# Row softmax on one core: one 192 KB array, loads of 3, 5, 8 and then 16 rows, stores of mostly 8 and at the end 16 rows, and the first two loads at the program's head on two queues

## The chip, the cores and the metric

One NeuronCore of a Trainium2 chip runs the kernel. DVE (VectorE) and ACT (ScalarE) compute. SP (SyncE) and ACT issue transfers, each on a queue of its own, and the core's 16 DMA engines carry them out. The metric is the device time of one execution in microseconds (us). All runs quoted are marked fast in the record, with the clock at 1.0. The kernel before took 162.68 us (median of 3 runs, 162.29 to 162.74).

## The reference

A softmax over the last dimension of an array of 16 x 1024 rows of 512 float32 values, 33.55 MB in and as much out:

```python
def reference(x: np.ndarray) -> np.ndarray:
    x_max = np.max(x, axis=-1, keepdims=True)
    exp_x = np.exp(x - x_max)
    return (exp_x / np.sum(exp_x, axis=-1, keepdims=True)).astype(np.float32)
```

Laid over 128 partitions, each partition has 128 rows of 2 KB. "Rows" below means rows per partition: a chunk of 8 rows is 128 x 8 x 2 KB = 2 MB.

## The kernel before

Sixteen chunks of 8 rows, twelve tiles. Each chunk goes through DVE (negated row maximum), ACT (exponential with that bias, and the row sum), DVE (reciprocal, then one scaling per row), and is stored. SP's queue issues the loads, ACT's queue the stores. The first load stands at the program's head, ahead of the start barrier.

```python
CHUNKS = [8] * 16
SLOTS = {8: 12}
# ... (first_load_at_the_head moves the first load before the barrier)
    def load(k):
        R = CHUNKS[k]
        tiles[k] = data.tile([P, R, d], F32, name=f"x{R}", tag=f"x{R}", bufs=SLOTS[R])
        nc.sync.dma_start(out=tiles[k], in_=src[k])
# ... rowmax(k): one reduce_max over the chunk;  exps(k): one activation per row
    def scale(k):
        R = CHUNKS[k]
        recip = stats.tile([P, R], F32, name=f"recip{R}", tag=f"recip{R}")
        nc.vector.reciprocal(out=recip, in_=sums[k])
        for r in range(R):
            nc.vector.tensor_scalar_mul(
                out=tiles[k][:, r, :], in0=tiles[k][:, r, :], scalar1=recip[:, r : r + 1])

    def store(k):
        nc.scalar.dma_start(out=dst[k], in_=tiles[k])

    with tc.manual_schedule():
        for k in range(K):
            load(k)
            rowmax(k)
            exps(k)
            if k >= 1:
                scale(k - 1)
                store(k - 1)
        scale(K - 1)
        store(K - 1)
```

## Time and profile before

| kernel before | value |
|---|---|
| time, median | 162.68 us |
| span of the profiled run | 160.6 us |
| DVE / ACT busy | 77% / 58% of the span |
| DMA engines busy (two queues) | 49.7% + 48.8% = 98.5% of 16 engines' span |
| bytes moved | 67.1 MB, 418 GB/s over the span |

From the page of the kernel before: the span; the busy time of the engines; the busy tenths of DVE and of the DMA engines in 40 slices of 4 us; the GB/s of each slice; the two queues (packets, MB, share of 16 engines' span; q1 is SP's queue, q10 is ACT's); and the chain that ended last, by engine.

```profile
span 160.6 us, 527 instructions
...
DVE 123.8 (77%) x160; ACT 93.2 (58%) x257; POOL 0.2 (0%) x4
...
DVE  0098799999999999885960089999999999967000
...
DMA  7999999999999999999999999999999999999993
GB/s 233 441 424 428 441 420 371 437 430 428 428 433 433 430 424 437 437 420 437 424 437 441 420 432 428 433 439 420 428 433 432 441 428 424 433 433 437 424 433 167
...
q1 hardware_dynamic: 2304, 33.56, 49.7%
q10 hardware_dynamic: 2304, 33.56, 48.8%
...
DMA 52%; DVE 31%; ACT 7%; SPq 1%; issue 1%; ACTq 0%; DVEq 0%
...
```

Read the DMA row first. It is 9 (90% or more) from the second slice to the last but one: the DMA engines are hardly ever without work. That is a bound, whatever the chain of waits says. DVE has 31% of the chain, but its row shows it idle in the middle of the program (the digits 8859600) while DMA stayed at 9.

The trace's packet records say how the engines spend this time. A packet is one contiguous run of one partition, here 16 KB, and 2048 packets per queue take 611 ns each (median). 16 engines x 16384 B / 611 ns is 429 GB/s, and 256 packets per engine are 156.4 us of the span of 160.6.

The two ends of the program, before. From the timeline, the first work on DVE (start, duration, engine, line, operation, operands, and in brackets the idle time before it and what ended it):

```profile
...
7.72 4.42 DVE L73 TENSOR_REDUCE shift<-x 128x8 f32<-128x4096 f32 x1 [7.72 <-DMA x<-in_x_dram]
```

From the DMA view of the stretch after 148 us, the last store (KB, us from issue to landing). It was issued at 149.0:

```profile
...
out_dram<-x ACTq DMA_DIRECT2D x1, 2048.0 KB, 10.8
```

Its 2 MB are 8 packets per engine, 4.9 us, yet it took 10.8 us. The rest is mostly older stores in line before it.

### The profile page before, as it was taken

The numbers are of one execution on the slowest core, as the hardware profiler recorded it, in microseconds if no ns is written. First come the engines' busy times: TensorE is split into PE (matmuls) and PEld (weight loads), VectorE is DVE, ScalarE is ACT, GpSimd is POOL, SyncE is SP. The second block draws the span as 40 slices with busy tenths as digits, with TensorE's granted clock in tenths as the row PEclk, the third lists the DMA queues.
The fourth block names the chain that finished last, engine by engine and source line by source line (L and its number), as shares of the span: only waits on it lengthen the run. The fifth ranks groups of instructions, "written<-read, shape, count | busy, mean of one in ns | idle before, by whom it ended". The sixth has DMA issues, their size and how long they took to land.

```text
span 160.6 us, 527 instructions
## 1 busy us (share of the span) xinstructions
DVE 123.8 (77%) x160; ACT 93.2 (58%) x257; POOL 0.2 (0%) x4
## 2 busy tenths in 40 slices
DVE  0098799999999999885960089999999999967000
ACT  0029985867777685076002987859595959592000
POOL 0000000000000000000000000000000000000000
DMA  7999999999999999999999999999999999999993
GB/s 233 441 424 428 441 420 371 437 430 428 428 433 433 430 424 437 437 420 437 424 437 441 420 432 428 433 439 420 428 433 432 441 428 424 433 433 437 424 433 167
DMA packets 4611, 67.14 MB, mean 418 GB/s; under 512 B 512, under 2 KB 512, under 8 KB 512
## 3 DMA queue, kind: packets, MB, share of 16 engines
q1 hardware_dynamic: 2304, 33.56, 49.7%
q10 hardware_dynamic: 2304, 33.56, 48.8%
q14 instruction: 3, 0.02, 0.0%
HBM read 33.55 MB, written 33.55 MB: 418 GB/s over the span
## 4 chain that ended last, share of the span: by engine, by line
DMA 52%; DVE 31%; ACT 7%; SPq 1%; issue 1%; ACTq 0%; DVEq 0%
DMA x<-in_x_dram 52%; DVE shift L73 16%; DVE x L93 14%; ACT x L79 7%; SPq L68 1%; DVE recip L91 1%; ACTq L100 0%; DVEq L137 0%; ACTq L79 0%
## 5 line engine op out<-in xcount | busy, mean ns | idle before, releaser
L79 ACT ACTIVATE x<-x,shift 128x512 f32<-128x512 f32 x128 | 90.5, 708 | 44.5 <-DVE shift L73 21.0
L73 DVE TENSOR_REDUCE shift<-x 128x8 f32<-128x4096 f32 x16 | 70.6, 4414 | 9.1 <-DMA x<-in_x_dram 9.1
L93 DVE TENSOR_SCALAR x<-x,recip 128x512 f32<-128x512 f32 x128 | 52.1, 481 | 0.6
L79 ACT ACTIVATION_READ_ACCUMULATOR x<-x,shift 128x1 f32 x128 | 23.9, 187 | 0.0
L91 DVE RECIPROCAL recip<-sums 128x8 f32<-128x8 f32 x16 | 3.1, 195 | 15.5 <-ACT x L79 15.5
L79 ACT ACT_TABLE_LOAD x1 | 1.3, 1283 | 7.8 <-DMA x<-in_x_dram 7.8
L126 POOL MEMSET const-bfloat16-1.0<- 128x1 bf16 x1 | 0.1, 101 | 0.0
L126 POOL MEMSET const-uint8-127<- 128x1 uint8 x1 | 0.1, 101 | 0.0
L126 POOL MEMSET const-float32-0.0<- 128x1 f32 x1 | 0.1, 98 | 0.2 <-issue 0.2
L126 POOL MEMSET const-float32-1.0<- 128x1 f32 x1 | 0.1, 98 | 0.0
## 6 DMA issues: line engine op xcount, KB each, us to landing
x<-in_x_dram SPq DMA_DIRECT2D x16, 2048.0 KB, 42.9
out_dram<-x ACTq DMA_DIRECT2D x16, 2048.0 KB, 17.7
```

The costliest lines, as they stand in the source:

```text
L68: nc.sync.dma_start(out=tiles[k], in_=src[k])
L73: nc.vector.reduce_max(out=shift[k], in_=tiles[k], axis=AX, negate=True)
L79: nc.scalar.activation(out=tiles[k][:, r, :], in_=tiles[k][:, r, :], func=EXP, bias=shift[k][:, r : r + 1], scale=1.0, accum_out=sums[k][: ...
L91: nc.vector.reciprocal(out=recip, in_=sums[k])
L93: nc.vector.tensor_scalar_mul(out=tiles[k][:, r, :], in0=tiles[k][:, r, :], scalar1=recip[:, r : r + 1],)
L126: nc = _bacc.Bacc("TRN2", target_bir_lowering=False, num_devices=1)
```

## The change

The intent: let compute begin sooner on a small first load, move more bytes per transfer and per packet once it runs, and start both queues at the program's head. All data lie in one array of 96 rows (192 KB per partition). Eight loads are issued at once (3, 5, 8, then five of 16 rows), and the last two 16-row loads reuse rows after the stores of earlier chunks. Compute still goes by groups of up to 8 rows. Three of the 16-row chunks are stored in halves; the last four are stored whole. The first three chunks are finished one after the other.

```diff
-CHUNKS = [8] * 16
-SLOTS = {8: 12}
+CHUNKS = [
+    (3, 0), (5, 3), (8, 8), (16, 16), (16, 32), (16, 48), (16, 64), (16, 80), (16, 0), (16, 16),
+]
+SBUF_ROWS = 96
+EARLY = 8
+AFTER_STORE = {2: [8], 3: [9]}
+GROUP = 8
+FINISH_BEFORE = (1, 2, 3)
+STORE_ROWS = {3: 8, 4: 8, 5: 8}
+ON_ACT = (0,)
+AT_HEAD = {mybir.EngineType.Activation: 1, mybir.EngineType.SP: 1}
...
     def load(k):
-        R = CHUNKS[k]
-        tiles[k] = data.tile([P, R, d], F32, name=f"x{R}", tag=f"x{R}", bufs=SLOTS[R])
-        nc.sync.dma_start(out=tiles[k], in_=src[k])
+        queue = nc.scalar if k in ON_ACT else nc.sync
+        queue.dma_start(out=place[k], in_=src[k])
...  (rowmax, exps and scale work on a group (k, a, b) of rows of place[k] in the same way)
+        if since is not None:
+            nc.scalar.dma_start(
+                out=dst[k][:, since:b, :], in_=place[k][:, since:b, :]
+            )
+        if b == CHUNKS[k][0]:
+            for later in AFTER_STORE.get(k, ()):
+                load(later)
...
+        for k in range(EARLY):
             load(k)
-            rowmax(k)
-            exps(k)
-            if k >= 1:
-                scale(k - 1)
-                store(k - 1)
-        scale(K - 1)
-        store(K - 1)
+        waiting = None
+        for g, (k, a, _, _) in enumerate(groups):
+            if waiting is not None and a == 0 and k in FINISH_BEFORE:
+                scale(waiting)
+                waiting = None
+            rowmax(g)
+            exps(g)
+            if waiting is not None:
+                scale(waiting)
+            waiting = g
+        scale(waiting)
```

More of the change, by code (lines that the diff above doesn't have):

```diff
@@ L10, with loads_at_the_head @@
 AX = mybir.AxisListType.X
-CHUNKS = [8] * 16
-SLOTS = {8: 12}
-def first_load_at_the_head(nc):
-    main, body = nc.main_func.blocks[0], nc.main_func.blocks[1]
-    dmas = [i for i in body.instructions if type(i).__name__ == "InstDMACopy"]
-    load = dmas[0]
-    assert load.engine == mybir.EngineType.SP
-    body.instructions.remove(load)
-    barrier = next(
-        n
-        for n, i in enumerate(main.instructions)
-        if i.engine == mybir.EngineType.SP and type(i).__name__ == "InstDrain"
-    )
-    main.instructions.insert(barrier, load)
+CHUNKS = [
[9 more added lines that the diff above has]
+AT_HEAD = {mybir.EngineType.Activation: 1, mybir.EngineType.SP: 1}
+def loads_at_the_head(nc):
+    main, body = nc.main_func.blocks[0], nc.main_func.blocks[1]
+    for engine, count in AT_HEAD.items():
+        loads = [
+            i
+            for i in body.instructions
+            if i.engine == engine and type(i).__name__ == "InstDMACopy"
+        ][:count]
+        barrier = next(
+            n
+            for n, i in enumerate(main.instructions)
+            if i.engine == engine and type(i).__name__ == "InstDrain"
+        )
+        for load in loads:
+            body.instructions.remove(load)
+        main.instructions[barrier:barrier] = loads
 @with_exitstack
@@ L40 @@
     nc = tc.nc
-    nc.at_finalize(first_load_at_the_head)
+    nc.at_finalize(loads_at_the_head)
     P = nc.NUM_PARTITIONS
@@ L46 @@
     n, d = x_flat.shape
-    assert n == P * sum(CHUNKS)
+    assert n == P * sum(R for R, _ in CHUNKS)
     src, dst, at = [], [], 0
-    for R in CHUNKS:
+    for R, _ in CHUNKS:
         for flat, views in ((x_flat, src), (out_flat, dst)):
@@ L58 @@
     stats = ctx.enter_context(tc.tile_pool(name="stats", bufs=4))
-    K = len(CHUNKS)
-    tiles = [None] * K
-    shift = [None] * K
-    sums = [None] * K
-    def load(k):
-        R = CHUNKS[k]
-        tiles[k] = data.tile([P, R, d], F32, name=f"x{R}", tag=f"x{R}", bufs=SLOTS[R])
-        nc.sync.dma_start(out=tiles[k], in_=src[k])
-    def rowmax(k):
-        R = CHUNKS[k]
-        shift[k] = stats.tile([P, R], F32, name=f"shift{R}", tag=f"shift{R}")
-        nc.vector.reduce_max(out=shift[k], in_=tiles[k], axis=AX, negate=True)
@@ L75, in exps @@
-    def exps(k):
-        R = CHUNKS[k]
-        sums[k] = stats.tile([P, R], F32, name=f"sums{R}", tag=f"sums{R}")
-        for r in range(R):
+    held = data.tile([P, SBUF_ROWS, d], F32, name="held")
+    place = [held[:, s : s + R, :] for R, s in CHUNKS]
+    groups = []
+    for k, (R, _) in enumerate(CHUNKS):
+        m = max(1, round(R / GROUP))
+        cuts = [R * i // m for i in range(m + 1)]
+        since = 0
+        for a, b in zip(cuts, cuts[1:]):
+            ends = b == R or b - since >= STORE_ROWS.get(k, R)
+            groups.append((k, a, b, since if ends else None))
+            since = b if ends else since
@@ new lines, with rowmax, exps @@
+    shift = [None] * len(groups)
+    sums = [None] * len(groups)
+    def load(k):
+        queue = nc.scalar if k in ON_ACT else nc.sync
+        queue.dma_start(out=place[k], in_=src[k])
+    def rowmax(g):
+        k, a, b, _ = groups[g]
+        shift[g] = stats.tile([P, b - a], F32, name="shift", tag="shift")
+        nc.vector.reduce_max(
+            out=shift[g], in_=place[k][:, a:b, :], axis=AX, negate=True
+        )
+    def exps(g):
+        k, a, b, _ = groups[g]
+        sums[g] = stats.tile([P, b - a], F32, name="sums", tag="sums")
+        for r in range(a, b):
@@ L79, in exps, with scale @@
             nc.scalar.activation(
-                out=tiles[k][:, r, :],
-                in_=tiles[k][:, r, :],
+                out=place[k][:, r, :],
+                in_=place[k][:, r, :],
                 func=EXP,
-                bias=shift[k][:, r : r + 1],
+                bias=shift[g][:, r - a : r - a + 1],
                 scale=1.0,
-                accum_out=sums[k][:, r : r + 1],
+                accum_out=sums[g][:, r - a : r - a + 1],
             )
-    def scale(k):
-        R = CHUNKS[k]
-        recip = stats.tile([P, R], F32, name=f"recip{R}", tag=f"recip{R}")
-        nc.vector.reciprocal(out=recip, in_=sums[k])
-        for r in range(R):
+    def scale(g):
+        k, a, b, since = groups[g]
+        recip = stats.tile([P, b - a], F32, name="recip", tag="recip")
+        nc.vector.reciprocal(out=recip, in_=sums[g])
+        for r in range(a, b):
@@ L93, in scale @@
             nc.vector.tensor_scalar_mul(
-                out=tiles[k][:, r, :],
-                in0=tiles[k][:, r, :],
-                scalar1=recip[:, r : r + 1],
-            )
-    def store(k):
-        nc.scalar.dma_start(out=dst[k], in_=tiles[k])
+                out=place[k][:, r, :],
+                in0=place[k][:, r, :],
+                scalar1=recip[:, r - a : r - a + 1],
+            )
+        if since is not None:
+            nc.scalar.dma_start(
+                out=dst[k][:, since:b, :], in_=place[k][:, since:b, :]
+            )
@@ L102 @@
+        if b == CHUNKS[k][0]:
+            for later in AFTER_STORE.get(k, ()):
+                load(later)
     with tc.manual_schedule():
-        for k in range(K):
+        for k in range(EARLY):
             load(k)
-            rowmax(k)
-            exps(k)
-            if k >= 1:
-                scale(k - 1)
-                store(k - 1)
-        scale(K - 1)
-        store(K - 1)
+        waiting = None
[8 more added lines that the diff above has]
+            waiting = g
```

## The prediction

> **What bounds it now.** The DMA engines, from start to end. Each works off one packet after another; a 16 KB packet takes 611 ns in the trace's packet records (16 x 16384 B / 611 ns = 429 GB/s). The 67.1 MB are 256 such packets per engine: 156.6 us of a span of 160.6. The page's slices agree: DMA busy 9 in all but the first and last, 420 to 440 GB/s except in slice 1 (233), 7 (371) and 40 (167). The Trainium skill ("DMA: Bandwidth & Descriptors", section "Where 436 GB/s comes from") gives 435 GB/s as the ports' ceiling; the trace has 98% of it. DVE (123.8 us busy, 77%) and ACT (58%) have slack. DVE is on the chain of waits (31%) only because the last stores queue: the last is issued at 149.0 and lands after 10.8 us, 4.9 of them its own transfer, so about 6 us of older stores lay before it.
>
> What is left to win is 160.6 - 156.6 = 4.0 us: about 1.0 before the first packet, 0.8 lost by slow first packets (0.9 to 1.9 us each), 0.5 at 22 to 26 us where the first store starts, 0.2 of instruction fetches, 0.3 of 512 semaphore packets, 1.1 after the last data.
>
> **What the change does.**
> - It moves the same bytes. 16-row loads have 32 KB runs per partition. An 8 KB packet takes 307 ns, a 16 KB one 611: a fixed cost of about 3 ns. 88 packets fewer per engine save 0.3 us at most; 9 semaphore packets fewer, at 9 ns, 0.1 us.
> - The 3-row load: first reduce at 4 to 5 us instead of 7.7. That helps DVE, which is not the bound.
> - Two queues at the head: the second load was issued at about 1 us, long before the first (4.9 us of transfer) was through. Nothing waited for it. The skill's section "Issuing engines are not separate DMA queues" says both queues run on the same 16 engines; the trace agrees (alternating packets, sum 429 GB/s). To be won is part of the 0.5 us that ACT's queue cost at its first use, if it was the queue and not the writing: I count 0.2.
> - 16-row stores at the end: the last needs 9.8 us, so it must be issued by about 149 or the DMA engines run dry. Working through the new order with measured durations (reduce 4.35 us and scales 3.4 per 8 rows, ACT 0.70 per row, the queues' packets in turn) I get loads done at about 111 us, DVE done at 145, the last store issued there and landing after some 14 us. No gap in DMA, 4 us of margin.
> - Waits for reused semaphores: one store of the sixth chunk waits for a load that DVE needs then anyway.
>
> **On the critical path:** 0.3 + 0.1 + 0.2 us, so about 162.2 us, range 161.2 to 163.4. Faster by over 2% would need under 159.4: less than the 156.6 us of packets plus 1.0, 1.1 and the 2 us between span and time. Faster 2%, same 95%, slower 3%.
>
> **What would show it.** DMA at 9 in all middle slices, 425 to 440 GB/s; first reduce at 4 to 5 us; DVE still 124 us busy but done by 142 to 148; 32 KB packets of about 1220 ns; the last store issued about 145 and landing after 13 to 15 us.
>
> **What would make it wrong.** A hole in DMA: at the end, if DVE falls 4 us behind (loads coming later because stores take a larger share), or while loads 9 and 10 wait for stores of the first four chunks. Larger packets that run below 429 GB/s. A start that costs more with small packets of 6 and 10 KB on two queues.

## The result

| | before | after |
|---|---|---|
| time, median of 4 runs | 162.55 us | 162.76 us |
| lowest to highest | 162.29 to 162.74 | 162.70 to 162.78 |
| span of the profiled run | 160.6 us | 161.0 us |

The ratio is 1.0013, with a 95% interval of 0.9996 to 1.0031: the same. A ratio here is the mean time of one kernel's fast runs over the mean of the other's fast runs of the same rounds, so it is not quite the ratio of the medians quoted.

The same lines of the page, of the changed kernel:

```profile
span 161.0 us, 516 instructions
...
DVE 123.9 (77%) x162; ACT 93.3 (58%) x257; POOL 0.2 (0%) x4
...
DVE  0048287079969999999999999999999999958000
...
DMA  7999999999999999999999999999999999996996
GB/s 254 430 489 391 421 417 391 449 398 481 409 411 458 456 391 436 409 476 415 440 415 464 432 423 419 456 389 423 444 468 399 464 440 399 456 448 277 391 391 261
...
q10 hardware_dynamic: 2016, 34.34, 49.8%
q1 hardware_dynamic: 1296, 32.77, 48.1%
...
DVE 71%; ACT 14%; DMA 5%; issue 2%; DVEq 0%; ACTq 0%
...
```

Two things differ. The chain is now 71% DVE. And the DMA row, which had no gap before, has two 6s near its end, with 277 GB/s in the slice of 144 to 148 us. The engines ran dry there. The table of stretches shows it more sharply. Its columns are the stretch, its length, the busy us of DVE, ACT and POOL with their instruction counts, the clock, the DMA share and GB/s (a packet is counted where it starts). First before, then after:

```profile
...
10.00:146.00 136.00, 118.53 (x153) 91.89 (x256) 0.00 (x0) 1.00 1.01 429
146.00:150.00 4.00, 2.96 (x8) 0.00 (x0) 0.00 (x0) 1.00 1.00 426
...
```

```profile
...
10.00:146.00 136.00, 119.64 (x155) 92.04 (x257) 0.00 (x0) 1.00 1.01 432
146.00:150.00 4.00, 2.97 (x8) 0.00 (x0) 0.00 (x0) 1.00 0.67 287
...
```

Up to 146 us the changed kernel is a little ahead. Counting each packet by the part of it that lies before a given time, the records have 61.73 MB moved by 146 us before and 61.96 MB after. Between 146 and 150 us it loses this and more: by 150 us it is 63.46 MB against 62.96. In the records the engines run out of packets one after the other between 148.0 and 149.0, and start again between 149.8 and 150.0 us.

The last store of the changed kernel, also issued at 149.0:

```profile
...
out_dram<-held ACTq DMA_DIRECT2D x1, 4096.0 KB, 11.1
```

This one line points to the hole. Twice the bytes need 8 x 1213 ns (the median of a 32 KB packet) = 9.7 us, and it took 11.1, of which 0.85 passed between the issue and its first packet. Nothing lay before it. In the kernel before, a store half as large took as long because it stood in line.

DVE therefore finished too late for a store of that size, though it is no later than before (both issue the last store at 149.0). The prediction had it finish at 145. The start shows why it did not. Timeline of the changed kernel, all engines (ACTq is the issue of a transfer on ACT's queue):

```profile
...
0.12 0.38 ACTq L96 DMA_DIRECT2D held<-in_x_dram  x1
...
8.72 1.75 DVE L101 TENSOR_REDUCE shift<-held 128x3 f32<-128x1536 f32 x1 [8.72 <-DMA held<-in_x_dram]
...
```

The first load has 3 rows instead of 8, and yet DVE starts at 8.72 us, later than the 7.72 of before. The DMA view of the first 9 us shows what became of it (queues: packets, MB, share; then issues: KB, us from issue to landing):

```profile
...
q1 hardware_dynamic: 209, 2.38, 70.2%
q10 hardware_dynamic: 144, 0.79, 21.0%
...
held<-in_x_dram SPq DMA_DIRECT2D x1, 1280.0 KB, 7.0
held<-in_x_dram ACTq DMA_DIRECT2D x1, 768.0 KB, 8.6
```

The first load's 0.79 MB on ACT's queue took 8.6 us. The packet records show two parts of this. It was issued at 0.12 us, but its first packet moved only at 2.68, while SP's queue began at 1.00 and had the engines alone until then (the DMA view from 0 to 2.6 us lists no packet of q10):

```profile
...
q1 hardware_dynamic: 40, 0.41, 64.5%
```

From then on the queues took turns, and its packets needed 5.0 us. SP's queue moved 2.38 MB in the first 9 us: the 5-row load and half of the 8-row load. The 5-row load landed first.

### The profile page after: what moved, and what is told of

Read it like the earlier page. It is cut to its first block, busy times and chain, and to the rows that moved or that the text cites. A ratio compares the mean times of both kernels' runs of the same rounds, so it can differ in the third digit from the quotient of the medians.

```text
span 161.0 us, 516 instructions
## 1 busy us (share of the span) xinstructions
DVE 123.9 (77%) x162; ACT 93.3 (58%) x257; POOL 0.2 (0%) x4
## 4 chain that ended last, share of the span: by engine, by line
DVE 71%; ACT 14%; DMA 5%; issue 2%; DVEq 0%; ACTq 0%
DVE shift L101 39%; DVE held L123 30%; ACT held L109 14%; DMA held<-in_x_dram 5%; DVE recip L121 2%; DVEq L175 0%; ACTq L109 0%
## 5 line engine op out<-in xcount | busy, mean ns | idle before, releaser
L109 ACT ACTIVATE held<-held,shift 128x512 f32<-128x512 f32 x128 | 90.5, 708 | 43.4 <-DVE shift L101 31.2
L101 DVE TENSOR_REDUCE shift<-held 128x8 f32<-128x4096 f32 (+2 forms) x17 | 70.6, 4160 | 8.7 <-DMA held<-in_x_dram 8.7
L123 DVE TENSOR_SCALAR held<-held,recip 128x512 f32<-128x512 f32 x128 | 52.2, 480 | 0.6
L109 ACT ACTIVATION_READ_ACCUMULATOR held<-held,shift 128x1 f32 x128 | 23.9, 187 | 0.0
L121 DVE RECIPROCAL recip<-sums 128x8 f32<-128x8 f32 (+2 forms) x17 | 3.3, 193 | 15.8 <-ACT held L109 15.8
## 6 DMA issues: line engine op xcount, KB each, us to landing
held<-in_x_dram SPq DMA_DIRECT2D x1, 2048.0 KB, 11.5
```

The lines of the kernel that those rows point to most:

```text
L101: nc.vector.reduce_max(out=shift[g], in_=place[k][:, a:b, :], axis=AX, negate=True)
L109: nc.scalar.activation(out=place[k][:, r, :], in_=place[k][:, r, :], func=EXP, bias=shift[g][:, r - a : r - a + 1], scale=1.0, accum_out=s ...
L121: nc.vector.reciprocal(out=recip, in_=sums[g])
L123: nc.vector.tensor_scalar_mul(out=place[k][:, r, :], in0=place[k][:, r, :], scalar1=recip[:, r - a : r - a + 1],)
```

## The experiments

All ran with five rounds beside the kernel before on the same chip, except the seventh (three); e5 left four times. e1 to e4 shared one chip, e5 to e8 a second, e9 and e10 a third, and the changed kernel was measured earlier, in rounds of its own with the kernel before. The kernel before had medians of 162.52, 162.50 and 162.29 us there, so across these groups compare the ratios. "e1" is called the repaired kernel below. The theory after the traces was this. The DMA engines bound both kernels. The changed kernel gains a few tenths on packets and start, and gives them back in one hole at the end. The hole is there because the first load lands late, DVE ends late, and the last store is large.

| run | median us | ratio to before (95%) | DVE ends at | last data moved at |
|---|---|---|---|---|
| changed kernel | 162.76 | 1.0013 (0.9996 to 1.0031) | 149.0 | 159.75 |
| e1_both_on_sp | 161.59 | 0.9946 (0.9934 to 0.9959) | 144.6 | 158.49 |
| e2_last_stores_8 | 161.70 | 0.9954 (0.9942 to 0.9967) | 148.8 | 158.72 |
| e3_sp_and_8 | 161.60 | 0.9952 (0.9939 to 0.9966) | 144.7 | 158.62 |
| e4_no_finish_first | 161.75 | 0.9956 (0.9943 to 0.9968) | 137.5 | 158.68 |
| e5_16k_runs | 166.85 | 1.0280 (1.0261 to 1.0299) | 152.8 | 163.73 |
| e6_all_stores_16 | 161.72 | 0.9958 (0.9944 to 0.9972) | 146.6 | 158.59 |
| e7_before_no_scale (wrong result) | 162.27 | 0.9991 (0.9977 to 1.0005) | - | - |
| e8_after_no_scale (wrong result) | 162.21 | 0.9986 (0.9973 to 0.9998) | - | 158.93 |
| e9_before_8k_runs | 163.54 | 1.0071 (1.0058 to 1.0084) | 149.3 | 160.65 |
| e10_16k_runs_stores_8 | 162.51 | 1.0011 (0.9997 to 1.0024) | 152.4 | 159.39 |

### e1: both head loads on SP's queue

```diff
-ON_ACT = (0,)
-AT_HEAD = {mybir.EngineType.Activation: 1, mybir.EngineType.SP: 1}
+ON_ACT = ()
+AT_HEAD = {mybir.EngineType.SP: 2}
```

> Theory A (the new kernel lost 1.7 us of DMA time in a hole at 148 to 150 us, because the 3-row load, on a queue of its own, took turns with the next loads and landed at 8.7 us): with both head loads on SP's queue the 3-row load lands at 4.3 to 5.2 us, DVE ends about 145, the last store is issued about 145, no hole, time 161.7 to 162.2 us, that is 0.5 to 1.0 under the changed kernel. Rival B (the hole comes from the three chunks done one after the other, 14 us of DVE idle, and not from the first landing): DVE still ends at 148 or later and the hole stays, 162.6 or more. Rival C (the hole does not set the time): DVE earlier, time the same within 0.2.

Measured: 161.59 us, 1.2 us under the changed kernel and 0.9 under the kernel before. The DMA view of its first 9 us:

```profile
...
q1 hardware_dynamic: 363, 3.33, 91.1%
...
held<-in_x_dram SPq DMA_DIRECT2D x1, 1280.0 KB, 6.9
held<-in_x_dram SPq DMA_DIRECT2D x1, 768.0 KB, 4.3
```

The 3-row load now lands after 4.3 us instead of 8.6, and DVE ends 4.4 us sooner. The 5-row load lands as soon as it did (6.9 against 7.0 us), so nothing was paid for it. From the page, the hole is gone:

```profile
span 159.7 us, 521 instructions
...
DMA  7999999999999999999999999999999999999993
...
```

And the last store, issued at 144.6 us, has a line before it again (14.2 us for 9.7 us of packets):

```profile
...
out_dram<-held ACTq DMA_DIRECT2D x1, 4096.0 KB, 14.2
```

Theory A holds in its end, with a gain 0.1 us larger than its range. Its reason, taking turns, is only part: of the 4.4 us by which the first reduce came sooner, 1.7 are the first packet (at 0.98 us against 2.68), 2.1 the turns (2.97 against 5.03 us from the first packet to the end of the last) and 0.6 the time from the last packet to the reduce. Why ACT's queue began later was not tested. It did so in all four kernels with that load (2.63 to 2.97 us), and no run put the 3-row load on SP's queue with the 5-row load on ACT's.

Rivals B (the landing doesn't matter) and C (the hole doesn't matter) fall for this edit.

### e2: the last chunks stored in halves

```diff
-STORE_ROWS = {3: 8, 4: 8, 5: 8}
+STORE_ROWS = {3: 8, 4: 8, 5: 8, 8: 8, 9: 8}
```

> Start untouched, the last two chunks stored in halves. Theory A: the first half of the last chunk is issued about 143 and fills the hole (4.9 us of transfer), DVE still ends at 149, time 161.7 to 162.2. Rival C: hole closed, time within 0.2 of 162.76. A rival D (the start on two queues itself costs DMA time): time stays above 162.5 whatever happens at the end.

Measured: 161.70 us. The start is as it was (DVE begins at 8.5 us) and DVE ends at 148.8, as late as in the changed kernel. But half of the last chunk was issued at 142.9 and bridged the gap; no idle time is left in the records between 144 and 157 us. A DVE that ends at 149 is harmless when the last store is 2 MB. That clears the two-queue start of any large cost of its own (rival D).

### e3: both edits

```diff
-STORE_ROWS = {3: 8, 4: 8, 5: 8}
+STORE_ROWS = {3: 8, 4: 8, 5: 8, 8: 8, 9: 8}
-ON_ACT = (0,)
-AT_HEAD = {mybir.EngineType.Activation: 1, mybir.EngineType.SP: 1}
+ON_ACT = ()
+AT_HEAD = {mybir.EngineType.SP: 2}
```

> Both edits. Theory A: no more than either alone, for there is one hole and each edit closes it: 161.7 to 162.2, within 0.2 of the better of the two. If the gains add up to over 1 us, A is wrong.

Measured: 161.60 us, no more than either alone. There was one hole, and each edit closes it.

### e4: the first chunks overlapped, the first load still on ACT's queue

```diff
-FINISH_BEFORE = (1, 2, 3)
+FINISH_BEFORE = ()
```

> Loads and stores as in the changed kernel, 3-row load still on ACT's queue, but the first chunks overlap as the later ones do. First reduce stays at 8.7. Theory A with B as its second part: DVE idles some 10 us less in the first 50 us, ends by 130 to 140, hole closed, 161.7 to 162.2. If only the late first landing mattered: DVE ends after 147 and the time stays at 162.6 to 162.9.

Measured: 161.75 us. The page's DVE and DMA rows:

```profile
...
DVE  0069969999999999999999999999999984300000
...
DMA  7999999999999999999999899899999999999993
...
```

DVE still starts late (9.35 us in this run), but has no more gaps while the first chunks go through ACT, and ends at 137.5. So the lateness had two causes, either of which would have been bearable: the first landing 4.4 us late (e1 against the changed kernel), and the first chunks done in series (11.5 us between the changed kernel's end of DVE and this one's). The series was the larger, but it was part of the prediction's order and is in e1 too, where DVE ends at 144.6; what came as a surprise was the first landing. What matters for a last store of 16 rows is only that it is issued before about 147: the older stores run out from 148.0 on, and its first packet moved 0.85 us after its issue (an estimate from the changed kernel; e6, where it is issued at 146.6, has no hole).

### e5: the 16-row transfers in runs of 16 KB

From the repaired kernel, with each 16-row transfer as two runs of 16 KB per partition (the same rows for loading and storing):

```diff
-            views.append(part.rearrange("(p r) d -> p r d", r=R))
+            if R == 16:
+                views.append(part.rearrange("(h p r) d -> p h r d", h=2, r=8))
+            else:
+                views.append(part.rearrange("(p r) d -> p r d", r=R))
...  (load and store use the same split of the array's rows)
```

> The repaired kernel (both head loads on SP's queue) with the same transfers, but the 16-row ones in two runs of 16 KB a partition instead of one of 32 KB: 16 KB packets at 611 ns in place of 88 packets per engine of 1213 ns, one more fixed cost of 9 ns for each. Theory A (what the change gained is this 9 ns): 88 x 9 ns = 0.8 us slower than the repaired kernel's 161.59, so 162.2 to 162.6, with no hole. Rival (the gain came from the start or from fewer transfers): 161.5 to 161.8.

Measured: 166.85 us. A clear miss: 5.3 us slower where 0.8 was expected, and by neither theory. The queues between 60 and 80 us, first of e5, then of the repaired kernel (packets, MB, share):

```profile
...
q1 hardware_dynamic: 286, 4.42, 51.8%
q10 hardware_dynamic: 286, 4.18, 48.8%
...
```

```profile
...
q1 hardware_dynamic: 201, 5.64, 65.4%
q10 hardware_dynamic: 205, 3.10, 36.1%
...
```

The packet counts of the two queues are nearly equal in both kernels (without the semaphores' packets 270 and 255, then 172 and 189). Each engine alternates between the queues packet by packet. (The records do not name the engine, but a packet starts within 6 ns of the end of the one before it on its engine; where only one fits, 97% of such pairs in e5 and 99% in e1 change the queue.) So a queue of 32 KB packets beside one of 16 KB packets gets about two thirds of the bandwidth, and with equal packets half. In e5 the last load was through at 130 us instead of 109. DVE then waited for loads (timeline, idle time in brackets):

```profile
...
111.86 4.42 DVE L107 TENSOR_REDUCE shift<-held 128x8 f32<-128x4096 f32 x1 [3.66 <-DMA held<-in_x_dram]
...
131.30 4.42 DVE L107 TENSOR_REDUCE shift<-held 128x8 f32<-128x4096 f32 x1 [3.88 <-DMA held<-in_x_dram]
```

It ended at 152.8 us, and the engines ran dry twice: for 1.0 us in front of the 16-row store issued at 139.2 (the digit 8 near the end of the DMA row) and for 3.9 us in front of the last one, issued at 152.8 (the digits 37). Together that is 4.9 of the 5.3 us:

```profile
...
DVE  0491950999699999999999999928998199967000
...
DMA  7999999999999999999999999999999998993795
...
```

So the 16-row loads do a second thing that the prediction's sum of gains does not name, though its working of the order, with "the queues' packets in turn" and loads done at about 111 us, contains it: their long packets give loads the right of way over the 8-row stores. The chunks of 16 rows with whole stores at the end work because of it.

### e10: e5 with all stores of 8 rows

```diff
-STORE_ROWS = {3: 8, 4: 8, 5: 8}
+STORE_ROWS = {k: 8 for k in range(3, 10)}
```

> e5 with all its stores of 8 rows. If e5 lost its time because loads and stores of equal packets share the engines one to one, so that the last load lands at 130 instead of 108, DVE ends at 153 and a 16-row store then finds the engines run dry: DVE still waits for loads and ends at 152 to 153, but the last store is 2 MB, so only a small hole is left and the time is 162.3 to 163.2 (the repaired kernel plus 0.8 us of packets plus what the last 2 MB store overhangs). If 16 KB runs in themselves are slow in these transfers: over 165.

Measured: 162.51 us, with DVE ending at 152.4 and no hole. This settles e5: the runs of 16 KB are not slow; the late loads followed by a large last store were. Against e3 (161.60), which has the same stores at the end, it lost 0.9 us: 72 packets more per engine are about 0.4 us at the 5 ns found in e9 below, and packets that took longer than the median of their size cost another 0.4 us per engine by the records (1.54 against 1.16). This division of the 0.9 us was not tested.

### e9: what a packet costs by itself

The kernel before, each transfer in two runs of 8 KB per partition, all else equal:

```diff
-            views.append(part.rearrange("(p r) d -> p r d", r=R))
+            views.append(part.rearrange("(h p r) d -> p h r d", h=2, r=R // 2))
...  (tiles seen as "p (h r) d -> p h r d" in load and store)
```

> The kernel before, every transfer in two runs of 8 KB a partition instead of one of 16 KB; same tiles, order, queues and number of transfers, and both queues still have packets of one size. 256 packets more per engine. If a packet's fixed cost is the 9 ns that 1213 - 2 x 602 = 9 and 611 - 602 = 9 give (and the 10 KB packets' 385 and the 6 KB packets' 234 ns): 8 KB packets take 310 ns, time 162.5 + 2.3 = 164.5 to 165.1. If it is the 3 ns of the prediction: 162.5 + 0.8, 163.1 to 163.5.

Measured: 163.54 us beside 162.29 of the kernel before in the same rounds, 1.15 us more by the ratio. That lies between the two expectations: 256 packets more per engine for 1.15 us are 4.5 ns each. The durations of the records mislead a little, because a packet's record overlaps the next one by some ns (the DMA share of full stretches reads 1.01). The pace of full stretches is the better measure, worked out as bytes moved over time: 427.9 GB/s with 8 KB packets (e9, 132 to 157 us), 431.2 with 16 KB (before, 130 to 157), 433.1 with 32 KB (e1, 124 to 155). As time per packet and engine that is 306.3, 608.0 and 1210.6 ns: a fixed cost of about 5 ns per packet.

### e6: every 16-row chunk stored whole

```diff
-STORE_ROWS = {3: 8, 4: 8, 5: 8}
+STORE_ROWS = {}
```

> The repaired kernel with every 16-row chunk stored whole: 24 pairs of 16 KB packets per engine become one each and three transfers go. Theory A: 24 x 9 ns = 0.2 us faster than 161.59, so 161.2 to 161.5, if no hole opens. Rival (packet size plays no part): 161.5 to 161.7.

Measured: 161.72 us, a miss by both readings of the packet cost (24 x 5 ns would be 0.1 us faster than e1; it is 0.1 slower). Differences of 0.1 us between these kernels are not resolved (the intervals of the two ratios overlap, and the runs are from two chips): the time ends with the slowest of 16 engines, and those differ by more. The larger stores also take the loads' right of way back. The last load is through at 123 us instead of 109, and DVE ends 2 us later.

### e7 and e8: the scalings taken away

Both give a wrong result: the 128 scalings, 52 us of DVE's work, are left out of the kernel before (e7) and of the changed kernel (e8).

```diff
         nc.vector.reciprocal(out=recip, in_=sums[k])
-        for r in range(R):
-            nc.vector.tensor_scalar_mul(...)
```

> Wrong result on purpose: the kernel before without its 128 scalings, 52 us of DVE's 124 taken away. If DMA alone bounds the kernel before: 162.2 to 162.8, as before. If DVE has a part in it (it is 31% of the chain): over 1 us faster.

Measured: 162.27 us, the same as before. Its page:

```profile
span 160.4 us, 414 instructions
...
DVE 72.8 (45%) x32; ACT 92.6 (58%) x257; POOL 0.2 (0%) x4
...
DMA  7999999999999999999999999999999999999994
...
```

DVE's busy time fell from 123.8 to 72.8 us and the time did not move: DVE's scalings do not bound the kernel before, though DVE had 31% of its chain, and its DMA row is as full as it was.

> Wrong result on purpose: the changed kernel without its scalings, start and stores otherwise as they are. Theory A (DVE is late for the last store only, and that costs the hole): no hole, the same 161.5 to 162.0 as the repaired kernel, no less, for the DMA engines then bound it. Rival (the changed kernel is bound by DVE altogether, 71% of the chain): under 160.

Measured: 162.21 us, with no hole, and 0.55 us under the changed kernel. That is 0.2 above the range given, and above the 161.6 to 161.75 of the others that closed the hole. Its data ended at 158.93 us against 158.49 in e1. Why was not settled; in the profiled run, the slowest of the five, all packets but one had ended by 157.97. But the rival is out: with 71% of the chain DVE could have been worth many microseconds, and taking 40% of its work away was worth half of one.

## Why the prediction was right

**The bound was right.** The prediction took the DMA engines for the limit of both kernels, from a DMA row without gaps and a sum of packet times. e7 confirms it: 51 us less of DVE, no difference. The ceiling it drew from the profile, at most 4 us to be won and most of that out of reach, is why "within 2%" was safe. No version here has a median below 161.59 us.

**The step that failed** is the prediction's "first reduce at 4 to 5 us instead of 7.7" and with it "DVE done at 145, the last store issued there ... No gap in DMA, 4 us of margin". The runs showed 8.72 us, 149.0 us, and a hole of about 1.9 us. The 4 to 5 us fit a first load that is ahead of the others, as on one queue. On a queue of its own its first packet moved 1.7 us later, and then it took turns packet by packet with the loads behind it. e1, which puts it in one line with the others, is the schedule that the prediction had described: first reduce at 4.3, last store issued at 144.6 and landing after 14.2 us ("13 to 15"). The prediction named such a hole among the things that would make it wrong, if DVE fell "4 us behind" (for another reason, later loads), and 4.0 us behind its 145 is what it was. Its limit for the last issue, "by about 149", was about 2 us too late as well: issued at 149.0, the store met engines that had been running dry since 148.0, and its first packet took another 0.85 us.

**The sizes.** The prediction summed 0.3 + 0.1 + 0.2 us of gain. By the packet records the changed kernel was 61.96 - 61.73 = 0.23 MB ahead at 146 us, which at 431 GB/s is 0.5 us. A gain was thus there, and the packet term is about 88 x 5 ns = 0.4 us, an estimate from the kernel before (e9); e5, which was to measure it in this kernel, was spoilt by the shares. The 0.2 us for ACT's queue was not tested by itself. Then came the hole: from 146 to 150 us the kernel before moved 1.73 MB and the changed one 1.00 MB, a loss of 1.7 us. What hid about 1 us of this is the end of the kernel before, where most engines were done near 158.4 us but one or two went on to 159.48. In the changed kernel all engines started the last store together after the hole and ended between 159.6 and 159.75. Why some engines were behind before was not tested. The sum is 0.2 us slower instead of 0.5 faster. Both lie within the forecast range. That the number was right was partly luck: a hole that the prediction had excluded cost 1.7 us, and the ragged end of the kernel before hid more than half of it.

**The two queues at the head** were judged to be free of gain, on the ground that nothing waited for the second load. They were worse than that: the split delayed the load that everything waits for. The Trainium skill ("DMA: Bandwidth & Descriptors", section "Issuing engines are not separate DMA queues") says that transfers from different engines run on the same 16 DMA engines and interleave. The prediction quoted it for the bandwidth and did not apply it to the first load. This trace agrees with it (2.38 MB and 0.79 MB in the first 9 us).

## What to carry to other kernels

When DMA is busy from end to end, count bytes and packets and expect little from moving compute; then make sure that the last store is small enough, or issued early enough, to follow the one before without a gap. Its time from issue to landing, set against its own packets, shows the slack at once. Put a transfer that everything waits for in the same queue as the ones behind it: on a second queue it takes turns with them, and here it also began 1.7 us later and landed after the larger load (8.6 us against 7.0). And remember that queues share by packets: the queue with the longer contiguous runs gets more.

## What the Trainium skill lacked or had wrong

- "DMA: Bandwidth & Descriptors", section "Where 436 GB/s comes from", says that for transfers between HBM and SBUF the HBM side (about 358 GB/s per core) binds. As it stands the sentence lacks a condition. Here one core moved 429 to 433 GB/s of such transfers, loads and stores mixed and stores alone, close to its 435 for the ports. This fits the page's own table of measurements, which has 425 for one large load on one core and says that the pair's other core was idle. No run here says what the chip's other cores did.
- The same page, section "Queues, rings and completion order", says that an engine takes turns between queues at packet granularity, but not what that does to shares when packets differ: 65.4% against 36.1% for 32 KB runs beside 16 KB ones (e1), 51.8% against 48.8% for equal ones (e5), and 5 us of time in this kernel. It also names 9 to 17 descriptors as typical for a packet; in these records a packet is one contiguous run of one partition, up to 32 KB, and with both queues at work an engine's records alternate between them one by one (97 to 99% of the pairs that can be told, in e5 and e1).
- The same page, section "Issuing engines are not separate DMA queues", says that a second issuing engine only saves issue time. It lacks the other side: a first load of 0.79 MB landed after 8.6 us on its own queue, whose first packet moved at 2.68 us, and after 4.3 us at the head of the common one, whose first packet moved at 0.98.
- The same page, section "Why small descriptors are slow (HBM only)", has a fixed cost of about 3 cycles per packet, and treats it as a matter for descriptors of a few hundred bytes. Here a fixed cost shows at 8 to 32 KB too: 427.9, 431.2 and 433.1 GB/s with packets of 8, 16 and 32 KB, about 5 ns each, and 1.15 us of time in e9. Whether it is the same cost, no run shows.
